# An encoder step in split fp32: values in two passes, gates normed at their banks, the second block's first weights behind its norm, the last chunk reordered

## The chip, the cores and the metric

One core of a Trainium2 chip runs the whole step as one launch. The metric is the device time of an execution in microseconds. The times are medians of several executions; a profile is of one execution.

## The reference

One layer of a streaming encoder on 512 prompt rows, 16 learned meta rows in front of them and 32 sample rows, width 1024:

```python
xp = half_step_ffn(xp, ffn1_norm, ffn1_w_gate, ffn1_w_up, ffn1_w_down)   # x + 0.5 * (silu(h@wg) * (h@wu)) @ wd
bp, cin_p, qp, ckv_p, kpe_p, gcp, gmp = project_inputs(rms_norm(xp, mix_norm), ...)  # h @ w_in_all
conv_branch = (b_gate * conv_y) @ w_conv_out
mla_branch = attn @ w_mla_out           # 16 heads, chunk-causal, keys and values expanded from 128 latents
merged = sigmoid(g_conv) * conv_branch + sigmoid(g_mla) * mla_branch
xp = xp + merged @ w_out_all
xp = half_step_ffn(xp, ffn2_norm, ...)
```

The same weights serve the sample rows (`xs`), which attend to a cache. Width of the blocks inside: 2816, heads 16 of 64 values and 96 key elements. Everything is float32, and the result must be right to nearly float32.

## The kernel before

Every float32 operand is split into a rounded part (hi) and the rest (lo): `split` casts on ScalarE and subtracts on VectorE or GpSimd. A product is three passes on TensorE (`mm3`, lines 161 to 164): hi·hi is L162, hi·lo of the moving operand L163, lo·hi L164. Activations stand with features on partitions and tokens in the free dimension, 544 or 560 columns in two halves of 272 or 280.

The stages, in order of the trace: the first feed-forward block to 384 us; its norm and the latents of keys and values to 423; attention with a filler to 935; gates, `w_mla_out` and `w_out` to 1039; the second block to the end.

A feed-forward block first makes one pair of 128-column blocks plainly (`plain`, its copies L277 and L278 empty the banks `acc`), and then 19 or 20 jobs, gate and up in turn, each of two column blocks by seven half-size products of sums (A11, A12, S2, S1, S3, A22, S4; `operands` makes the weights' sums on VectorE (tile `ws`) and casts them (`yh`, `yl`, `zh` for A22), `job` multiplies). Between the products S3 and A22 of a job the bank `b` must be read by u3, a copy with the sign changed (L385, ScalarE, tile `kept`), before A22 adds to the same bank. Between jobs stand the chunks of the down projection (`down`): `part` multiplies pairs of activations `ah`, `al`, `close` adds the result to `y`. The last chunk has three pairs, and its first two output blocks are opened before the last pair is done.

In attention each pair of heads expands keys K and values V (`expand_kv`; the keys are normed on VectorE, L976 to L984, and transposed on TensorE, L1033). Each head multiplies scores (`score`), takes the softmax (`soft`), transposes the probabilities (L1204) into four tiles pTh, pTl of 512, 384, 256 and 128 columns, and the meta rows' into `pM` (L1209, L1212 to L1214), and multiplies the values into a bank `t` (64 partitions, 512 columns), three passes a tile, and last VM by pM (L1220). L1222 copies the bank to `at`.

Beside attention runs a filler (`stream`): 48 units of 48 matmuls, each in two halves of 24 into the two `f` banks. 24 units are for the convolution, 16 for the branch gates and 8 for `w_conv_out`; `spilled` copies the last two kinds from the bank to `b1` (L903, ScalarE) and out to memory. A gate stands there without its norm R2. The late stage loads it (`gate`), multiplies by R2 on GpSimd (in three pieces, L73), takes the sigmoid (L1270), and merges both branches in `sg` (L1282, L1283), which is split into `mh` and `ml` for `w_out`.

The order on each engine is made by a scheduler that simulates the program's time line; the code's order, the buffers and added order dependencies (NoSync: on one engine, without a semaphore) are its input. So an edit at one place can change the order at others.

## Time and profile before

| | us |
|---|---|
| median of 3 executions | 1433.81 (1432.49 to 1439.06) |
| profiled execution, its own time | 1433.34 |
| its span, first to last instruction | 1431.6 |
| TensorE busy, share | 1388.9, 97% |
| VectorE busy, share | 1010.9, 71% |
| ScalarE busy, share | 650.7, 45% |
| GpSimd busy, share | 477.4, 33% |
| mean granted TensorE clock | 0.996 |

The profiled time is the span and what lies around it, 1.7 us. Busy shares are averages over stages of different kinds, and a busy TensorE is made of pipelined passes, so the distance from one start to the next tells what a pass costs.

### The profile page before, as it was taken

How to read it: one execution, taken by the hardware profiler on the slowest of the kernel's cores; microseconds unless marked ns; L12 is line 12 of the kernel's file. 1: busy time of each engine (PE TensorE's matmuls, PEld its weight loads, DVE VectorE, ACT ScalarE, POOL GpSimd, SP SyncE). 2: the span in 40 equal slices, each digit the busy share in tenths (PEclk: the TensorE clock that was granted, in tenths of full speed). 3: DMA queues.
4: the chain of work that ended last, by engine and by line, in shares of the span. 5: the costliest groups of instructions: out<-in, count | busy, mean ns of one | idle time of the engine just before them, and what ended most of it. 6: DMA issues, size and time to landing. Idle time of an engine off the chain costs nothing.

```text
span 1431.6 us, 26658 instructions
## 1 busy us (share of the span) xinstructions
PE 1388.9 (97%) x10679; PEld 1356.4 (95%) x10679; DVE 1010.9 (71%) x1708; ACT 650.7 (45%) x1218; POOL 477.4 (33%) x695
## 2 busy tenths in 40 slices
PE   7999999999999999999999999999999999999998
PEld 6999999999899999998999999998999999999998
DVE  5887877877666665956955757545977787878754
ACT  6644343535324454454554556533544343534341
POOL 1011111202286864645623424167811021111110
PEclk9999999999999999999999999999999999999999
DMA  6332323323243222222432234365442332324213
GB/s 172 89 118 73 105 76 102 103 76 90 87 123 94 84 79 77 71 61 57 120 91 72 84 115 150 110 179 165 137 117 89 89 104 74 118 75 122 67 45 96
DMA packets 215635, 141.64 MB, mean 99 GB/s; under 512 B 6415, under 2 KB 202914, under 8 KB 215510
## 3 DMA queue, kind: packets, MB, share of 16 engines
q1 hardware_dynamic: 215510, 139.93, 33.4%
q8 instruction: 84, 1.38, 0.4%
q14 instruction: 41, 0.34, 0.1%
HBM read 124.15 MB, written 15.76 MB: 98 GB/s over the span
## 4 chain that ended last, share of the span: by engine, by line
PE 82%; POOL 6%; DVE 5%; DMA 3%; issue 2%; ACT 1%; SPq 0%; POOLq 0%; ACTq 0%; DVEq 0%
PE b L162 10%; PE b L163 9%; PE b L164 9%; PE acc L162 8%; PE acc L163 8%; PE acc L164 7%; PE f L162 6%; PE f L163 6%; PE f L164 6%; POOL sg L73 2%; POOL sq L73 1%; PE t L162 1%; PE late L163 1%; PE t L1204 1%; PE late L162 1%
## 5 line engine op out<-in xcount | busy, mean ns | idle before, releaser
L73 POOL TENSOR_TENSOR al<-tu,ah 128x187 fp32r<-128x187 f32 (+3 forms) x108 | 98.5, 945 | 568.5 <-issue 340.6
L116 ACT CAST wh<-wr 128x1024 fp32r<-128x1024 f32 (+2 forms) x166 | 167.7, 1019 | 226.1 <-PE acc L163 121.1
L162 PE MATMUL f<-xh,wh 128*128 128x272 f32 (+1 forms) x816 | 240.0, 294 | 2.3 <-DVE ext L874 1.6
L164 PE MATMUL f<-xh,wl 128*128 128x272 f32 (+1 forms) x816 | 238.9, 293 | 0.0
L163 PE MATMUL f<-xl,wh 128*128 128x272 f32 (+1 forms) x816 | 238.5, 292 | 0.0
L163 PE MATMUL acc<-al,wh 128*128 128x280 f32 (+1 forms) x704 | 203.7, 291 | 3.4 <-DVE al L117 3.4
L162 PE MATMUL acc<-ah,wh 128*128 128x280 f32 (+1 forms) x704 | 203.0, 292 | 1.8 <-ACT ah L116 0.9
L164 PE MATMUL acc<-ah,wl 128*128 128x280 f32 (+1 forms) x704 | 202.8, 291 | 0.5 <-DVE wl L117 0.5
L73 POOL TENSOR_TENSOR wl<-wr,wh 128x256 fp32r<-128x256 f32 x196 | 151.8, 804 | 150.0 <-ACT wh L116 122.1
L117 DVE TENSOR_TENSOR wl<-wr,wh 128x1024 fp32r<-128x1024 f32 (+2 forms) x116 | 141.8, 1229 | 32.7 <-ACT wh L116 29.5
L162 PEld LDWEIGHTS f<-xh,wh 128*128 128x128 f32 x816 | 154.7, 190 | 3.5 <-ACT wh L116 1.8
L163 PEld LDWEIGHTS f<-xl,wh 128*128 128x128 f32 x816 | 154.7, 190 | 0.4
L164 PEld LDWEIGHTS f<-xh,wl 128*128 128x128 f32 x816 | 154.7, 190 | 0.5
L163 PEld LDWEIGHTS acc<-al,wh 128*128 128x128 f32 x704 | 132.5, 188 | 4.1 <-DVE al L117 4.0
L163 PE MATMUL b<-xsl,yh 128*128 128x272 f32 (+1 forms) x468 | 135.6, 290 | 0.0
L162 PE MATMUL b<-xsh,yh 128*128 128x272 f32 (+1 forms) x468 | 135.6, 290 | 0.0
L164 PE MATMUL b<-xsh,yl 128*128 128x272 f32 (+1 forms) x468 | 135.4, 289 | 0.0
L162 PEld LDWEIGHTS acc<-ah,wh 128*128 128x128 f32 x704 | 131.7, 188 | 3.2 <-ACT ah L116 1.4
L164 PEld LDWEIGHTS acc<-ah,wl 128*128 128x128 f32 x704 | 132.0, 188 | 0.7 <-DVE wl L117 0.7
L117 DVE TENSOR_TENSOR yl<-ws,yh 128x1024 fp32r<-128x1024 f32 x78 | 100.8, 1292 | 36.8 <-ACT yh L116 36.2
L116 ACT CAST yh<-ws 128x1024 fp32r<-128x1024 f32 x78 | 81.9, 1051 | 95.1 <-PE b L163 83.0
L467 DVE SCALAR_TENSOR_TENSOR tu<-acc,R 128x560 f32<-128x560 f32 (+1 forms) x80 | 58.2, 730 | 46.5 <-PE acc L164 46.3
(361 smaller groups left out, 3868.2 us busy)
## 6 DMA issues: line engine op xcount, KB each, us to landing
wr<-in_w_in_all_dram SPq DMA_DIRECT2D x43, 512.0 KB, 4.3
wr<-in_ffn_w_down_dram SPq DMA_DIRECT2D x32, 512.0 KB, 3.5
wr<-in_ffn_w_gate_dram SPq DMA_DIRECT2D x24, 512.0 KB, 3.8
wr<-in_ffn_w_up_dram SPq DMA_DIRECT2D x23, 512.0 KB, 5.1
wq<-in_ffn_w_up_dram SPq DMA_DIRECT2D x20, 512.0 KB, 4.2
wq<-in_ffn_w_gate_dram SPq DMA_DIRECT2D x19, 512.0 KB, 4.0
wr<-in_ffn_w_down_dram SPq DMA_DIRECT2D x16, 384.0 KB, 3.3
gt_dram<-b SPq DMA_DIRECT2D x16, 272.0 KB, 2.0
```

Source lines behind the costliest of these rows:

```text
L73: last = op(out[:, lo:hi], a[:, lo:hi], b[:, lo:hi])
L116: a = S.copy(hi, src)
L117: return a, (E or V).tensor_sub(lo, src, f(hi))
L162: PE.matmul(out, a[0], b[0], start=start, stop=False, skip_group_check=onto)
L163: PE.matmul(out, a[0], b[1], start=False, stop=False, skip_group_check=onto)
L164: PE.matmul(out, a[1], b[0], start=False, stop=stop, skip_group_check=onto)
L467: V.scalar_tensor_tensor(t, ps[:, :, :n], 0.5, Rv, op0=ALU.mult, op1=ALU.mult)
L1204: PE.transpose(ps[:, (t - j) * P : (t - j + 1) * P], pw[:, a : a + P], ident)
```

## The change

Six edits: the values' hi and lo halves lie in one tile VV, the product of a head takes two passes a tile into a bank of 128 partitions, and a ScalarE copy and a VectorE addition join the halves; the branch gates are multiplied by R2 when they leave the `f` bank, on VectorE, and not in the late stage; the second block's first summed weights get an order dependency behind the last copy of its norm (`spread` returns it; `before(1)` passes it on); the second cast of a job's weights gets one behind u3; in the first block the condition for the first job reads `combine` and not `made`; the last chunk's parts are cut at the first pair and not before the last.

```diff
--- before.py
+++ after.py
@@ -290,7 +290,7 @@
                     S.activation(g, g, AF.Silu)
                     V.tensor_mul(u, u, g)
                     split(ah[:, 0], al[:, 0], u)
-                    ready = [c(ready) for c in combine]
+                    ready = [c(ready) for c in combine] or ready
             g, u = rows(), rows()
             V.tensor_mul(two(g), ps[0][:, :, :n], Rv)
             S.activation(g, g, AF.Silu)
@@ -321,6 +321,8 @@
                 )
             return raw
 
+        made_hi = []
+
         def operands(raw, after=None):
 
             def parts(*args):
@@ -339,6 +341,7 @@
             steps.append(V.tensor_add(s2, s1, a11))
             steps.append(V.tensor_add(s4, s2, a12))
             views = A + B + parts(sums[1], pool, "y", 3) + [a22]
+            made_hi[:] = steps[-2:-1]
             if after:
                 for j, x in enumerate(steps):
                     tc.add_manual_dep(x.ins, after[j > 1].ins.name, NOSYNC, reason="later")
@@ -382,7 +385,7 @@
             product(d, S1, X1)
             product(b, S3, X3, False)
             u3 = pool.tile([P, n], F32, tag="kept", name="kept", bufs=4)
-            S.mul(u3, b, -1.0)
+            G["u3"] = S.mul(u3, b, -1.0)
             V.tensor_sub(out(0)[:, h[1]], u3, d)
             yield
             product(b, A22, X4, False)
@@ -475,9 +478,11 @@
             opened = []
             for m in range(ahead):
                 ps = open_(m)
-                part(ps, m, 0, nf - 2)
+                part(ps, m, 0, 2)
+                if m == 0:
+                    yield
+                part(ps, m, 2, nf - 2)
                 opened.append(ps)
-                yield
             for m in range(ahead):
                 part(opened[m], m, nf - 2, nf)
                 close(opened[m], m)
@@ -494,9 +499,9 @@
         jobs = [(make, w, p) for p in range(1, NF // 2) for make, w in ((gate_job, wg), (up_job, wu))]
         made = plain(0)
         ops, raws = None, [None]
-        if not made:
+        if not combine:
             raws = [fetch(*jobs[0][1:])]
-            ops = operands(raws[0])
+            ops = operands(raws[0], [made] * 2)
         raws.append(fetch(*jobs[1][1:]))
         pending = None
         ready = None
@@ -513,7 +518,9 @@
             next(g)
             pending = g
             if x + 1 < len(jobs):
-                ops = operands(raws[x + 1], made and x == 0 and made[-2:])
+                ops = operands(raws[x + 1], combine and x == 0 and made[-2:])
+                if "u3" in G:
+                    tc.add_manual_dep(made_hi[0].ins, G["u3"].ins.name, NOSYNC, reason="later")
             if x + 2 < len(jobs):
                 raws.append(fetch(*jobs[x + 2][1:]))
             if d:
@@ -896,11 +903,15 @@
                     dma(cy_dram[c], b1)
             return win(OB + c * P), META, NL, use
 
-        def spilled(w, dst):
+        def spilled(w, dst, scaled):
             def use(q, ps, x):
                 if q == 0:
                     st["b1"] = pool.tile([P, L], F32, tag="b1", name="b1")
-                S.copy(st["b1"][:, q * NL : (q + 1) * NL], ps)
+                b1 = st["b1"][:, q * NL : (q + 1) * NL]
+                if scaled:
+                    V.tensor_mul(b1, ps, R2[:, x])
+                else:
+                    S.copy(b1, ps)
                 if q == 1:
                     dma(dst, st["b1"])
             return w, META, NL, use
@@ -909,9 +920,10 @@
             units = []
             for c in range(KD):
                 units += [conv_c(c), conv_v(c), conv_b(c)]
-            units += [spilled(win(OGC + m * P), gt_dram[m]) for m in range(2 * KD)]
+            units += [spilled(win(OGC + m * P), gt_dram[m], True) for m in range(2 * KD)]
             units += [
-                spilled(i["w_conv_out"][0, :, m * P : (m + 1) * P], cb_dram[m]) for m in range(KD)
+                spilled(i["w_conv_out"][0, :, m * P : (m + 1) * P], cb_dram[m], False)
+                for m in range(KD)
             ]
             block = lambda u: load([u[0]], E=GP)
             w = block(units[0])
@@ -956,8 +968,8 @@
                 ],
             )
             K = pool.tile([P, 7, 2, QK], F32, tag="K", name="K", bufs=2)
-            Vh = pool.tile([P, 7, 2, VD], F32R, tag="Vh", name="Vh", bufs=2)
-            Vl = pool.tile([P, 7, 2, VD], F32R, tag="Vl", name="Vl", bufs=2)
+            VV = pool.tile([P, 7, 2, 2, VD], F32R, tag="VV", name="VV", bufs=2)
+            Vh, Vl = VV[:, :, :, 0], VV[:, :, :, 1]
             for t in range(7):
                 ps = bank("acc")[:, : 2 * P]
                 c = slice(t * P, (t + 1) * P)
@@ -985,7 +997,7 @@
                 K[:, :, :, NOPE:], kpe[:, :, None, :].to_broadcast([P, 7, 2, ROPE]),
                 rk[:, :, :, None].to_broadcast([P, 7, 2, ROPE]),
             )
-            return K, Vh, Vl, VM
+            return K, VV, VM
 
         def expand_q(g, us):
 
@@ -1077,7 +1089,7 @@
                 dst, src, AF.Exp, bias=nm[rows, col : col + 1], accum_out=sm[rows, col : col + 1]
             )
 
-        def sample_values(Vh, Vl, at, pS):
+        def sample_values(VV, at, pS):
 
             n = 2 * SAMP
             ps = bank("t")
@@ -1092,9 +1104,9 @@
             ov = bank("t")
             for j, (t, r) in enumerate(((5, P), (6, P), (4, SAMP))):
                 mm3(
-                    ov[:n, :P],
+                    ov[:n, :P].rearrange("p (h c) -> p h c", c=VD),
                     (sTh[:r, j], sTl[:r, j]),
-                    tuple(v[:r, t].rearrange("p h c -> p (h c)") for v in (Vh, Vl)),
+                    (VV[:r, t, :, 0], VV[:r, t, :, 1]),
                     j == 0,
                     j == 2,
                 )
@@ -1140,7 +1152,7 @@
             if e == 0:
                 at = pool.tile([P, L], F32, tag="at", name="at")
                 pS = pool.tile([P, KP], F32, tag="pS", name="pS")
-            K, Vh, Vl, VM = KV[pr]
+            K, VV, VM = KV[pr]
             pw = pws[e]
             nm = pool.tile([P, 5], F32, tag="nm", name="nm", bufs=2)
             sm = pool.tile([P, 5], F32, tag="sm", name="sm", bufs=2)
@@ -1213,15 +1225,18 @@
             V.tensor_sub(pM[32:64], ps[:32], f(pM[:32]))
             S.copy(pM[64:], ps[:32])
             fill(1.0)
-            ov = bank("t")[:VD]
+            ov = bank("t")
             for j in range(NQ):
-                vj = (Vh[:, j, e], Vl[:, j, e])
-                mm3(ov[:, 512 - NT[j] :], vj, (pTh[j], pTl[j]), j == 0, False)
-            PE.matmul(ov, VM[:, e], pM, start=False, stop=True)
+                vj = VV[:, j, e].rearrange("p s c -> p (s c)")
+                for x in (pTh[j], pTl[j]):
+                    PE.matmul(ov[:, 512 - NT[j] :], vj, x, start=j == 0 and x is pTh[j], stop=j == NQ - 1 and x is pTl[j])
+            PE.matmul(ov[:VD], VM[:, e], pM, start=False, stop=True, skip_group_check=True)
             half = slice(e * VD, (e + 1) * VD)
-            V.tensor_copy(at[half, SAMP:], ov)
+            other = slice((1 - e) * VD, (2 - e) * VD)
+            S.copy(at[half, SAMP:], ov[other])
+            V.tensor_add(at[half, SAMP:], ov[half], at[half, SAMP:])
             if e:
-                sample_values(Vh, Vl, at, pS)
+                sample_values(VV, at, pS)
                 if pr < KD - 1:
                     dma(at_dram[pr], at)
                 else:
@@ -1266,7 +1281,6 @@
         def gate(m):
             sg = late.tile([P, L], F32, tag="sg", name="sg", bufs=4)
             dma(sg, gt_dram[m])
-            GP.tensor_mul(sg, sg, R2[:, META:])
             S.activation(sg, sg, AF.Sigmoid)
             return sg
 
```

Where the instructions stand. ScalarE, in the middle of the second block: `yh` is the cast of the summed weights `ws`, `ah` that of an activation, `zh` that of A22's weights; the instruction with ACTIVATE and `kept` is u3 (L385), and the COPY to `kept` are the copies p1 and u2. Before:

```order
L365 COPY kept<-b 128x272
L116 CAST ah<-tu 128x544
L116 CAST yh<-ws 128x1024
L385 ACTIVATE kept<-b 128x272
L365 COPY kept<-b 128x272
L116 CAST zh<-wq 128x512
L389 ACTIVATE tg<-b 128x272
```

And after the change, where u3 is L388:

```order
L368 COPY kept<-b 128x272
L116 CAST ah<-tu 128x544
L388 ACTIVATE kept<-b 128x272
L116 CAST yh<-ws 128x1024
L368 COPY kept<-b 128x272
L116 CAST zh<-wq 128x512
L392 ACTIVATE tg<-b 128x272
```

The cast `yh` has moved from ahead of u3 to behind it. Between the last pass of S3 and the first of A22 on TensorE there are, over the 39 jobs, 22 to 31 passes in most; in the changed order ten jobs have 0, 0, 0, 1, 2, 2, 2, 2, 4 and 4.

VectorE at the second block's start: L336 to L340 make the weights' sums, L563, L565 (L570, L572 after) and L174 to L180 the norm, L278 empties a bank of `plain`. Before:

```order
L117 TENSOR_TENSOR zl<-wq,zh 128x512
L339 TENSOR_TENSOR ws<-ws,wr 128x512
L117 TENSOR_TENSOR yl<-ws,yh 128x1024
L340 TENSOR_TENSOR ws<-ws,wr 128x512
L336 TENSOR_TENSOR ws<-wq 128x512
L563 TENSOR_SCALAR ms<-b 128x4
L565 TENSOR_SCALAR ms<-b 32x1
L174 TENSOR_SCALAR r_77<-ms 128x5
L117 TENSOR_TENSOR yl<-ws,yh 128x1024
L178 TENSOR_TENSOR nra<-r_77 128x5
L278 COPY tu<-acc 128x544
```

After:

```order
L117 TENSOR_TENSOR zl<-wq,zh 128x512
L570 TENSOR_SCALAR ms<-b 128x4
L572 TENSOR_SCALAR ms<-b 32x1
L174 TENSOR_SCALAR r_77<-ms 128x5
L178 TENSOR_TENSOR nra<-r_77 128x5
L179 SCALAR_TENSOR_TENSOR nrb<-nra,ms 128x5
L180 SCALAR_TENSOR_TENSOR r_77<-nrb,r_77 128x5
L178 TENSOR_TENSOR nra<-r_77 128x5
L179 SCALAR_TENSOR_TENSOR nrb<-nra,ms 128x5
L278 COPY tu<-acc 128x544
```

The sums and both `yl` have moved behind the norm; L278 stands in the middle of the norm's short operations.

TensorE at the end of attention, last head: `f` are the filler's passes, `t<-ident,pw` the transpositions of the probabilities (32x128 those of the meta rows). Before:

```order
L163 MATMUL f<-xl,wh 128x272
L1204 MATMUL t<-ident,pw 128x128 x2
L164 MATMUL f<-xh,wl 128x272
L162 MATMUL f<-xh,wh 128x272
L1204 MATMUL t<-ident,pw 128x128
L163 MATMUL f<-xl,wh 128x272
...
L164 MATMUL f<-xh,wl 128x272
L1209 MATMUL t<-ident,pw 32x128 x4
L162 MATMUL t<-pTh,Vh 64x512
L163 MATMUL t<-pTl,Vh 64x512
L164 MATMUL t<-pTh,Vl 64x512
```

After:

```order
L164 MATMUL f<-xh,wl 128x272
L1216 MATMUL t<-ident,pw 128x128 x10
L1221 MATMUL t<-ident,pw 32x128 x4
L1232 MATMUL t<-pTh,VV 128x512
L1232 MATMUL t<-pTl,VV 128x512
L1232 MATMUL t<-pTh,VV 128x384
L1232 MATMUL t<-pTl,VV 128x384
```

The filler's passes between the transpositions are gone: from the values of the last head but one to the end 18 of them are left, before 70. Two passes a tile stand where three stood.

## Rows read from the trace of the kernel before

**Rows 1.** The page's first part: busy time of each engine, share of the span, instructions.

```profile
PE 1388.9 (97%) x10679; PEld 1356.4 (95%) x10679; DVE 1010.9 (71%) x1708; ACT 650.7 (45%) x1218; POOL 477.4 (33%) x695
```

**Rows 2.** The table of stretches: from and to, length, busy time and instructions of PE, PEld, DVE, ACT and POOL, granted clock of TensorE, share of the DMA engines, GB/s. The stages of attention and behind it, fifty microseconds of attention, and one microsecond behind a stop.

```profile
423.00:935.00 512.00, 503.11 (x3838) 481.81 (x3838) 336.93 (x800) 259.78 (x642) 246.24 (x393) 1.00 0.31 90
935.00:1039.00 104.00, 100.50 (x773) 99.94 (x773) 67.15 (x74) 44.95 (x60) 83.78 (x110) 0.97 0.55 161
700.00:750.00 50.00, 50.00 (x391) 47.52 (x391) 33.27 (x82) 27.18 (x77) 17.73 (x27) 1.00 0.32 94
994.00:995.00 1.00, 1.00 (x7) 1.00 (x6) 0.64 (x2) 0.00 (x0) 0.38 (x1) 0.50 0.94 286
```

**Rows 3.** The list of TensorE's waits: who waited, for what, us in all, times, longest.

```profile
PE b L162 <- ACT kept L385: 6.5, 9, 1.3
PE acc L1033 <- DVE K L984: 4.1, 2, 2.7
PE acc L163 <- DVE al L117: 3.4, 3, 1.4
PE late L162 <- ACT mh L116: 2.9, 1, 2.9
PE acc L162 <- DVE tu L278: 2.4, 1, 2.4
PE t L1220 <- ACT pM L1214: 1.5, 1, 1.5
```

**Rows 4.** The timeline of TensorE at the last head: start, duration, engine, line, operation, operands, shapes, how many. The values' passes and two groups of transpositions.

```profile
929.58 0.39 PE L164 MATMUL t<-pTh,Vl 128*64 128x512 f32 x1
929.81 0.34 PE L162 MATMUL t<-pTh,Vh 128*64 128x384 f32 x1
929.98 0.34 PE L163 MATMUL t<-pTl,Vh 128*64 128x384 f32 x1
930.57 0.28 PE L164 MATMUL t<-pTh,Vl 128*64 128x256 f32 x1
930.69 0.22 PE L162 MATMUL t<-pTh,Vh 128*64 128x128 f32 x1
930.75 0.22 PE L163 MATMUL t<-pTl,Vh 128*64 128x128 f32 x1
...
922.07 0.60 PE L1204 MATMUL t<-ident,pw 128*128 128x128 f32 x4
927.57 0.27 PE L1204 MATMUL t<-ident,pw 128*128 128x128 f32 x1
```

**Rows 5.** Groups of instructions by line and form: operands, shapes, how many, then busy us and mean ns of one, then the idle time ahead of them. Two of weight loads, two copies in attention, and a filler's eviction with the norm.

```profile
L163 PEld LDWEIGHTS t<-pTl,Vh 128*64 128x64 f32 x64 | 8.6, 135 | 2.0
L163 PEld LDWEIGHTS f<-xl,wh 128*128 128x128 f32 x816 | 154.7, 190 | 0.4
L1222 DVE COPY at<-t 64x512 f32<-64x512 f32 x16 | 10.9, 678 | 7.9 <-PE t L1220 7.5
L1212 ACT CAST pM<-t 32x512 fp32r<-32x512 f32 x16 | 9.1, 571 | 3.1 <-PE t L1209 2.9
L892 DVE TENSOR_TENSOR b<-f,R 128x272 f32<-128x272 f32 x16 | 7.0, 437 | 10.3 <-PE f L164 9.7 <-POOL VM L971 0.6
```

**Rows 6.** The timelines of GpSimd and of TensorE in the late stage (columns as in Rows 4; in brackets the idle time ahead and what ended it).

```profile
985.51 5.81 POOL L73 TENSOR_TENSOR sg<-sg,R 128x181 f32<-128x181 f32 x9
...
993.46 0.60 PE L163 MATMUL late<-ml,wh 128*128 128x272 f32 x1 [0.48 <-DVE ml L117]
993.86 0.43 PE L164 MATMUL late<-mh,wl 128*128 128x272 f32 x1
...
996.35 0.38 PE L163 MATMUL late<-ml,wh 128*128 128x272 f32 x1
```

**Rows 7.** The timelines of ScalarE and TensorE around u3, in a job of the second block and in the last job of the first.

```profile
1214.07 1.05 ACT L116 CAST yh<-ws 128x1024 fp32r<-128x1024 f32 x1 [3.59 <-PE b L163]
1215.02 0.39 ACT L385 ACTIVATE kept<-b 128x272 f32<-128x272 f32 x1
1215.46 0.39 PE L162 MATMUL b<-xsh,zh 128*128 128x272 f32 x1 [1.06 <-ACT kept L385]
...
370.33 0.28 PE L164 MATMUL b<-xsh,yl 128*128 128x280 f32 x1
371.11 0.40 PE L162 MATMUL b<-xsh,zh 128*128 128x280 f32 x1 [0.49 <-ACT kept L385]
```

**Rows 8.** The timelines of VectorE and TensorE at the second block's start.

```profile
1053.22 1.23 DVE L117 TENSOR_TENSOR yl<-ws,yh 128x1024 fp32r<-128x1024 f32 x1 [0.18 <-ACT yh L116]
1054.44 0.72 DVE L278 COPY tu<-acc 128x544 f32<-128x544 f32 x1
...
1055.21 0.39 PE L162 MATMUL acc<-xh,wh 128*128 128x272 f32 x1 [2.43 <-DVE tu L278]
```

**Rows 9.** The timelines of TensorE and VectorE around one pair's keys: the last pass of the expansion, the reduction, the last product of the keys, the first transpositions.

```profile
642.95 0.28 PE L164 MATMUL acc<-wkh,kvl 128*128 128x256 f32 x1
...
649.87 1.09 DVE L976 TENSOR_REDUCE vk<-sqk 128x14 f32<-128x896 f32 x1
...
658.80 1.14 DVE L984 TENSOR_TENSOR K<-kpe,rk 128x448 f32<-128x448 f32 x1
...
659.99 0.64 PE L1033 MATMUL acc<-ident,K 128*96 128x128 f32 x4 [2.74 <-DVE K L984]
```

## The prediction

> **What bounds the kernel now.** Read the page's list of engines first: TensorE is busy 97% of the span, VectorE 71%, ScalarE 45%, GpSimd 33% [rows 1]. Then the table by stages: TensorE stands still for 8.9 us of the 512 in the attention stage (512.00 − 503.11) and for 3.5 us of the 104 in the stage behind it [rows 2]. So the time is mostly the number of passes that TensorE makes, at about 128 ns each (50.00 us by 391 matmuls [rows 2]), and a gain is either a pass less or one of the few waits. The list of TensorE's waits gives their places: 6.5 us on the sign-changed copy u3 (`kept`, L385), 4.1 on the finished keys (L984), 2.9 on the merged rows `mh`, 2.4 on a bank's copy at the second block's start (L278), 3.4 on the last pair's `al`, 1.5 on `pM` at the end of attention [rows 3].
>
> **The change, part by part.**
>
> *Values in two passes.* The hi half and the lo half of the values stand side by side in one stationary operand, so a pass over pTh multiplies both. The pass Vh·pTl stays and brings Vl·pTl with it; the third pass (L164) goes. Start-to-start in the timeline, it takes 0.23 us at 512 columns (929.58 to 929.81), 0.17 at 384 (929.81 to 929.98), 0.12 at 256 (930.57 to 930.69) and 0.06 at 128 (930.69 to 930.75) [rows 4]: 0.58 us a head, 16 heads, −9.3 us.
> What the two left cost more: their load has 128 columns and not 64, and such loads take 190 ns against 135 [rows 5]. Behind 256 columns and more (spacing 0.12 us and up) nothing should show, since the filler's 272-column passes with 128-wide loads run at 128 ns. Behind 128 columns the nearest row is the transposition with a 128-wide operand: four take 0.60 us, one 0.27, so 0.11 us each and not 0.06 [rows 4]. Two passes, 16 heads, 0.05 us more: +1.7 us (bounds 0, if the load hides, and 1.7).
> The two halves of the result must be added: a ScalarE copy of 64x512 (nearest row 571 ns, L1212 [rows 5]) and then a VectorE add, where one VectorE copy stood (678 ns [rows 5]). The chain to `at` gets 0.6 us longer; for 15 heads nobody waits, since the bank of the values is read long after. The last head's part of it is under the tail below.
>
> *Gates take the norm at their banks.* From the late stage 48 GpSimd products go (16 gates in three pieces); nine of them take 5.81 us in a row just before the stall [rows 6], and the row `mh` waits for them through a sigmoid. In the chain of work that ended last they are what TensorE stood for: 2.9 us on `mh` [rows 3] and 0.48 more at 993.46 for `ml` [rows 6]. After that stop the granted clock is 0.50 of full, the 1.2 GHz level [rows 2]: eleven passes from 993.86 to 996.35 take 2.49 us [rows 6] where 11 × 0.128 is 1.41, so 1.1 us more. With the products gone a gate is one transfer and one sigmoid, and the merged row is ready while the row before it is multiplied. Sum −4.5 us (bounds: −3.4 if the clock falls anyway, −5.2 if the stage's other stops go too).
> The price: 32 evictions of 128x272 move from ScalarE to VectorE, 32 × 437 ns (L892 [rows 5]) = 14 us of VectorE, between some 700 and 850 us. VectorE is busy 33.27 us of 50 there [rows 2], so the work fits; but each eviction frees one of two `f` banks, and its place behind a longer operation costs when it is later than a half unit of 24 passes (3.1 us). I take +1 us (bounds 0 and 3; the 16 evictions of this kind in `before` made TensorE wait never).
>
> *The next job's second cast behind u3.* At 1214.07 ScalarE takes a 1.05 us cast `yh` and only then u3, and TensorE stops 1.06 us; at 370.33, with no cast between and no matmuls to cover it, u3 alone makes 0.78 us from start to start instead of 0.13 [rows 7]. So the stop has two parts: 0.65 us less whatever passes cover it, and the cast. The nine waits of before come to 6.5 us idle; at 371.11 start-to-start says 0.65 where idle says 0.49, so 0.16 more each, 7.9 us. In the changed order the cast is never ahead of u3 (it is in 33 of 39 jobs before). What is left is u3 alone, in jobs with few passes between S3 and A22: 0, 0, 0, 1, 2, 2, 2, 2, 4 and 4 passes, priced max(0, 0.65 − 0.128 each): 3 × 0.65 + 0.52 + 4 × 0.39 + 2 × 0.14 = 4.3 us. Sum −3.6 us (bounds −6, if the other engines let the cover stay as before, and +1, if the cast comes late for S2: about 3.1 us from its sum to its use, against at least 3.7 of cover).
>
> *Second block's first summed weights behind the norm.* At 1053.22 VectorE takes `yl` (1.23 us) ahead of the bank copy L278 at 1054.44, and TensorE stops 2.43 us for that [rows 8]. In the changed order two sums and two `yl` stand later, but the short norm operations and ScalarE's two casts remain ahead of the copies; I take −1.0 of the 2.4 (bounds −0.5 and −1.5).
>
> *Last chunk in another order.* The passes that need the last pair still follow its last S4 product with nothing between on TensorE, in both orders; the waits on `al` (3.4 us [rows 3]) stay. 0.
>
> *What moves because the rest does.* (a) Keys. From the last expansion pass (642.95) VectorE's and GpSimd's chain takes to 659.94 (reduction at 649.87, L984 from 658.80 for 1.14), and TensorE's cover is short by 2.74 us [rows 9]. Priced with row spacings, the cover of the eight pairs is 21.5, 16.9, 14.4, 14.0, 13.5, 12.3, 13.6 and 12.2 us before, and 21.5, 14.1, 14.2, 14.3, 13.5, 14.1, 14.6 and 12.5 after, with 0.4 to 1.7 us more VectorE work inside five of the chains (an eviction, an addition). The second pair, whose chain takes 16.4 us, loses 2.8 us of cover: +2.3; the pairs at the margin about +1.7. Sum +4 (bounds 0 and +8). (b) Tail. The filler ends earlier: 18 of its passes are left for the last head instead of 70, so 52 × 0.128 = 6.7 us of cover are gone there, and ten transpositions, four of `pM` and the values stand in one piece. In the bare chain (casts of pT, then `pM` in three steps of 0.57 to 0.68, then the 0.6 us copy in `at`) 1.5 us were open already [rows 3]. Sum +3 (bounds +1 and +6.7).
>
> **Sum.** −9.3 + 1.7 − 4.5 + 1 − 3.6 − 1.0 + 4 + 3 = −8.7. The profiled execution took 1433.34 us (span 1431.6), 0.5 under the median of 1433.81. 1433.34 − 8.7 = 1424.6, said as **1425 us**.
>
> **The rivals.**
> *The attention stage gives the passes back.* TensorE is 98% busy there, but keys and tail are chains of other engines, with a length of their own. For it: both lose cover in the new order. Against it: only two of eight pairs waited before. With the upper bounds of (a) and (b): 1425 + 4 + 3.7 = 1433, no change.
> *The whole gain stays.* The new waits are covered, as the 8.9 us of idle time of that stage says of most waits now. (a), (b) and evictions near 0 instead of +8: 1417; with u3's −6 1414.
> *Slower: VectorE becomes the bound between 700 and 850 us.* All gate evictions now queue behind casts' differences of up to 1.2 us on VectorE. It decides once each half unit is late by more than its two banks cover: at 0.33 us each the gain of the values is eaten (32 × 0.33 = 10.6), at 0.8 us late each it adds 26 us: some 1448. For it: 33 of 50 us busy and 14 more to come. Against: no wait on L892 in the list.
> *The weight loads set the pace.* If none of the 54 ns more of a load is hidden, 8 passes × 16 heads × 0.054 = 6.9 us in place of 1.7: 1430. Against it: passes of 272 columns hide loads of 128 columns. The Trainium skill ("TensorE: Matmul & The Clock Gate", section "LDWEIGHTS (loading the stationary operand)") speaks for it: a load's time goes by the columns of its operand alone, not by its rows, so doubling them doubles it, 53 to 107 ns by its formula. The trace agrees on the growth (135 to 190 ns), less than double.
>
> **How the numbers follow.** The forecast 0.45, own range 1420 to 1429; the whole gain 0.25; given back 0.18; loads 0.06; slower 0.06. A measurement of this kernel can tell about 0.5%, 7 us: faster means under 1426.6. Of the forecast's range two thirds lie below (0.30), all of the whole gain (0.25), and a few of the others: faster 0.57. Slower (above 1441) 0.06; same 0.37. The range 1412 to 1434 leaves out the slower case, the end of "given back" and a little below: 2 in 10.
>
> **What would show it.** Values: eight passes a head, 64 matmuls fewer, spacings 0.23, 0.17, 0.12 and 0.11; TensorE's busy time some 8 us less in the attention stage. Gates: no wait on `mh` and clock 1.00 behind 989; no wait of a filler pass on the new evictions. u3: some ten waits on `kept` of under 0.5 us, none of 1 us. Second block: L278's wait near 1.4. Keys: the wait on L984 at 8 us, tail idle 3 us longer than now. Wrong it would be if the attention stage's idle time does not grow (then 1417) or grows by more than the passes saved (then 1433 and above), or if VectorE's evictions appear among TensorE's waits.

## The result, and the profile after

The changed kernel takes 1424.8 us (median of 4 executions, 1424.04 to 1424.93) where the kernel before takes 1433.94: ratio 0.9929, interval 0.9904 to 0.9953, so 0.7% faster. The forecast was 1425. The total is right, and the profile shows that it is right for partly wrong reasons. By the forecast's terms attention was to get 0.4 us longer, and it got 4.3 shorter; the two feed-forward blocks were to give 4.6 us, and together they gave nothing. The two misses cancel. (Two executions that were very much slower than all others, 1968 us of the kernel before and 2701 us of the kernel e12 below, are left out of the medians.)

The profiled execution took 1424.04 us, its span is 1422.3. First the page's list of engines of the changed kernel, to be held against [rows 1]:

```profile
PE 1384.5 (97%) x10615; PEld 1355.5 (95%) x10615; DVE 1012.2 (71%) x1740; ACT 648.6 (46%) x1202; POOL 443.8 (31%) x647
```

64 matmuls fewer, 32 VectorE instructions more, 48 on GpSimd fewer. Then the table of stretches, cut at the first filler pass, at the first pass of `w_mla_out` and at the first pass of the second block:

```profile
0.00:423.88 423.88, 409.27 (x3084) 402.12 (x3084) 315.59 (x442) 188.13 (x285) 92.59 (x132) 1.00 0.35 102
423.88:932.05 508.17, 497.35 (x3776) 479.80 (x3777) 346.44 (x832) 259.44 (x626) 246.78 (x393) 0.99 0.31 91
932.05:1030.18 98.13, 98.13 (x770) 98.13 (x770) 62.32 (x73) 44.16 (x58) 50.37 (x61) 0.98 0.57 169
1030.18:1422.30 392.12, 379.78 (x2990) 375.48 (x2988) 287.86 (x394) 156.83 (x233) 54.02 (x63) 1.00 0.31 91
```

Cut at the same passes, the four stretches of the kernel before are 423.05, 512.44, 103.17 and 392.90 us. So attention gave 4.3 us, the late stage 5.0, the second block 0.8, and the part up to attention took 0.8 more. From the list of TensorE's waits of the changed kernel, against [rows 3] (some rows are left out):

```profile
PE b L162 <- ACT kept L388: 5.0, 14, 0.5
PE acc L163 <- DVE al L117: 3.5, 3, 1.6
PE t L1216 <- DVE pTl L117: 3.3, 2, 2.1
PE acc L162 <- ACT wh L116: 2.1, 3, 0.9
PE t L1216 <- DVE pw L1181: 1.3, 1, 1.3
PE f L162 <- DVE b L912: 1.3, 1, 1.3
PE acc L1045 <- DVE K L996: 1.1, 1, 1.1
PE t L162 <- DVE at L1237: 1.0, 1, 1.0
PE acc L162 <- DVE tu L278: 0.8, 1, 0.8
```

The wait on `mh` is gone, the one on keys nearly; the nine waits on u3 have become fourteen, shorter ones; three are new: pTl and `pw` in attention, and `b` (L912), a gate's eviction on VectorE.

**Values.** TensorE's timeline at an ordinary head, the last seven of its eight passes and the instruction behind them:

```profile
637.81 0.39 PE L1232 MATMUL t<-pTl,VV 128*128 128x512 f32 x1
638.04 0.34 PE L1232 MATMUL t<-pTh,VV 128*128 128x384 f32 x1
638.21 0.34 PE L1232 MATMUL t<-pTl,VV 128*128 128x384 f32 x1
638.39 0.28 PE L1232 MATMUL t<-pTh,VV 128*128 128x256 f32 x1
638.50 0.28 PE L1232 MATMUL t<-pTl,VV 128*128 128x256 f32 x1
638.63 0.22 PE L1232 MATMUL t<-pTh,VV 128*128 128x128 f32 x1
638.69 0.28 PE L1232 MATMUL t<-pTl,VV 128*128 128x128 f32 x1
638.80 0.33 PE L162 MATMUL s<-kTh,qTh 100*128 100x264 f32 x1
```

From start to start 0.23 us at 512 columns, 0.17, 0.11 to 0.13, 0.06, as before the change [rows 4]. Only the last pass keeps TensorE 0.11 us (638.69 to 638.80) and not 0.06.

**Keys of the fourth pair.** The last expansion pass, the reduction, the last product and the transpositions, on TensorE and VectorE:

```profile
641.32 0.28 PE L164 MATMUL acc<-wkh,kvl 128*128 128x256 f32 x1
...
646.66 1.07 DVE L988 TENSOR_REDUCE vk<-sqk 128x14 f32<-128x896 f32 x1
...
655.84 0.62 DVE L996 TENSOR_TENSOR K<-kpe,rk 128x448 f32<-128x448 f32 x1
...
657.06 0.60 PE L1045 MATMUL acc<-ident,K 128*96 128x128 f32 x4
```

The chain from 641.32 to 656.46 is 15.1 us; before it was 17.0 [rows 9]. The reduction comes 5.3 us behind the expansion instead of 6.9, and TensorE does not wait for the keys. But it waits for something else within this stretch, the differences pTl of the head beside it:

```profile
653.37 0.44 PE L1216 MATMUL t<-ident,pw 128*128 128x128 f32 x2 [1.15 <-DVE pTl L117]
```

**Second block's start.** VectorE's copy and TensorE, against [rows 8]: the stop of 2.43 us is one of 0.82.

```profile
1044.34 0.72 DVE L278 COPY tu<-acc 128x544 f32<-128x544 f32 x1 [0.28 <-PE acc L164]
1045.12 0.40 PE L162 MATMUL acc<-xh,wh 128*128 128x272 f32 x1 [0.82 <-DVE tu L278]
```

**u3.** ScalarE and TensorE in a job of the second block, against [rows 7]:

```profile
1080.47 2.00 ACT L116 CAST wh<-wr 128x1024 fp32r<-128x1024 f32 x2 [2.34 <-DMA wr<-in_ffn_w_down_dram]
1082.38 0.39 ACT L388 ACTIVATE kept<-b 128x272 f32<-128x272 f32 x1
...
1082.81 0.40 PE L162 MATMUL b<-xsh,zh 128*128 128x272 f32 x1 [0.48 <-ACT kept L388]
```

`yh` is behind u3 now. Two casts `wh`, of other weights (`w_down`), stand ahead of it, and ScalarE had stood idle for 2.34 us until their transfer landed.

**Tail of attention.** TensorE, ScalarE and VectorE at the last head:

```profile
921.11 0.93 PE L1216 MATMUL t<-ident,pw 128*128 128x128 f32 x7
924.18 0.79 PE L1216 MATMUL t<-ident,pw 128*128 128x128 f32 x3 [2.14 <-DVE pTl L117]
925.91 0.76 PE L1232 MATMUL t<-pTh,VV 128*128 128x512 f32 x1
926.46 0.63 PE L1232 MATMUL t<-pTl,VV 128*128 128x512 f32 x1
...
921.22 1.05 ACT L116 CAST wh<-wr 128x1024 fp32r<-128x1024 f32 x1 [1.11 <-issue]
922.30 1.23 DVE L117 TENSOR_TENSOR wl<-wr,wh 128x1024 fp32r<-128x1024 f32 x1 [1.52 <-ACT wh L116]
```

And stretches of the changed kernel at the last head, at the start of the late stage and in its middle, with the granted clock in the third column from the end:

```profile
927.00:928.00 1.00, 1.00 (x6) 1.00 (x5) 0.61 (x1) 0.35 (x1) 0.00 (x0) 0.50 0.01 2
934.00:935.00 1.00, 1.00 (x6) 1.00 (x5) 0.00 (x0) 0.49 (x1) 0.00 (x0) 0.50 0.05 10
985.00:990.00 5.00, 5.00 (x42) 5.00 (x41) 4.18 (x6) 1.57 (x2) 0.00 (x0) 1.00 0.37 109
```

Behind the stop at 922 the last head's values run at the 1.2 GHz level (0.55 us from 925.91 to 926.46, and not 0.31). The late stage still begins with some 3 us at half clock (the second line); in the kernel before, 936 to 938 has 0.50 too. From 937 on nothing stops and the clock is whole, where the kernel before stopped for `mh` and then ran at half clock again [rows 2, 6].

### The profile page after: what moved, and what is told of

Same layout as the page of the kernel before. It is cut to its first block, busy times and chain, and to the rows that moved or that the text cites. A ratio compares the mean times of both kernels' runs of the same rounds, so it can differ in the third digit from the quotient of the medians.

```text
span 1422.3 us, 26510 instructions
## 1 busy us (share of the span) xinstructions
PE 1384.5 (97%) x10615; PEld 1355.5 (95%) x10615; DVE 1012.2 (71%) x1740; ACT 648.6 (46%) x1202; POOL 443.8 (31%) x647
## 4 chain that ended last, share of the span: by engine, by line
PE 82%; DVE 6%; DMA 3%; POOL 3%; ACT 2%; issue 2%; SPq 0%; POOLq 0%; DVEq 0%; ACTq 0%
PE b L162 8%; PE b L163 8%; PE b L164 8%; PE acc L162 8%; PE acc L164 8%; PE acc L163 8%; PE f L162 6%; PE f L163 6%; PE f L164 6%; PE late L164 2%; PE late L162 2%; PE late L163 2%; DMA wr<-in_ffn_w_down_dram 2%; PE t L1232 1%; POOL sq L73 1%
## 5 line engine op out<-in xcount | busy, mean ns | idle before, releaser
L117 DVE TENSOR_TENSOR wl<-wr,wh 128x1024 fp32r<-128x1024 f32 (+2 forms) x116 | 138.3, 1202 | 42.6 <-ACT wh L116 35.2
L116 ACT CAST yh<-ws 128x1024 fp32r<-128x1024 f32 x78 | 81.5, 1045 | 19.9 <-PE b L163 15.5
L162 PE MATMUL b<-xh,wh 128*128 128x272 f32 (+1 forms) x312 | 90.5, 290 | 0.0
```

What stands on the lines that cost most here:

```text
L116: a = S.copy(hi, src)
L117: return a, (E or V).tensor_sub(lo, src, f(hi))
L162: PE.matmul(out, a[0], b[0], start=start, stop=False, skip_group_check=onto)
```

## The experiments

Each kernel was timed against the kernel before on the same chip, where the kernel before took 1433.6 to 1434.7 us. In the table: the median, the ratio, and from the profiled execution the four stretches cut as above. Where two kernels of the table are compared, the ratios are the better measure, since the chips differ.

| kernel | median us | ratio (interval) | to attention | attention | late | second block |
|---|---|---|---|---|---|---|
| before | 1433.94 | | 423.1 | 512.4 | 103.2 | 392.9 |
| changed | 1424.80 | 0.9929 (0.9904, 0.9953) | 423.9 | 508.2 | 98.1 | 392.1 |
| e1 values alone | 1430.51 | 0.9970 (0.9960, 0.9980) | 425.4 | 508.1 | 102.5 | 393.5 |
| e2 gates alone | 1431.18 | 0.9977 (0.9967, 0.9986) | 424.6 | 514.0 | 98.6 | 392.3 |
| e3 order behind u3 alone | 1439.99 | 1.0045 (1.0028, 1.0062) | 424.1 | 512.2 | 106.1 | 395.3 |
| e4 norm first alone | 1432.67 | 0.9985 (0.9975, 0.9994) | 422.8 | 510.9 | 103.1 | 391.2 |
| e9 changed, no order behind u3 | 1422.89 | 0.9926 (0.9911, 0.9940) | 423.8 | 507.6 | 98.1 | 392.1 |
| e6 changed + cover | 1420.49 | 0.9913 (0.9898, 0.9928) | 421.7 | 507.6 | 97.9 | 390.5 |
| e7 changed + tail | 1422.67 | 0.9924 (0.9908, 0.9941) | 423.3 | 506.0 | 98.5 | 393.8 |
| e8 changed + cover + tail | 1418.58 | 0.9894 (0.9878, 0.9911) | 420.6 | 506.1 | 98.5 | 391.3 |
| e10 as e8, no order behind u3 | 1424.37 | 0.9927 (0.9912, 0.9942) | 422.0 | 506.9 | 98.9 | 394.6 |
| e11 changed, gates as before | 1433.33 | 0.9993 (0.9983, 1.0002) | 423.1 | 510.8 | 106.4 | 393.0 |
| e12 changed, last chunk as before | 1424.69 | 0.9932 (0.9915, 0.9949) | 424.7 | 508.4 | 98.4 | 392.5 |
| e13 changed again | 1423.97 | 0.9921 (0.9905, 0.9938) | 425.2 | 506.6 | 98.3 | 394.1 |

The rows of the changed kernel and of e13 are the same program: a stretch of one profile differs by up to 2 us from that of another. So stretches are read together with the waits in them.

**e1, values alone.** The hunks on VV, `sample_values` and the head's end, on the kernel before:

```diff
-            Vh = pool.tile([P, 7, 2, VD], F32R, tag="Vh", name="Vh", bufs=2)
-            Vl = pool.tile([P, 7, 2, VD], F32R, tag="Vl", name="Vl", bufs=2)
+            VV = pool.tile([P, 7, 2, 2, VD], F32R, tag="VV", name="VV", bufs=2)
...
```

> The kernel before with the values in two passes alone. Theory A (the sum of the prediction): the passes saved are given back by keys and tail, -9.3 + 1.7 + 4 + 3 = about -0.6 us: 1433 us, the attention stage (first filler pass to first pass of w_mla_out, 512.4 us before) at 512. Theory B (from the changed kernel's trace, where 128-wide loads cost 0.05 us a head and the waits on keys fell from 4.1 to 1.1 us): the passes are worth 8.5 us and the other engines' chains take at most 3 of it back: 1426 to 1429 us, the stage at 504 to 508.

Attention is 508.1 us, 4.4 shorter, and the kernel 0.3% faster: theory B on the stage. The key chains are those of the changed kernel (the second pair 14.2 us, the fourth 15.1, where before has 16.4 and 17.0), so the shorter chains came with the values and not with the gates. The total is 1430.5, above theory B's 1426 to 1429. What its profile shows beside is a wait of 2.6 us on `xh` in attention, with half clock behind it (858 to 861), and half clock at 28 to 31 and at 384 to 386, all three at whole clock in the kernel before.

**e2, gates alone.** `spilled(..., True)` for the gates and no product in `gate`, on the kernel before.

> The kernel before with the gates normed at their banks alone. Theory A: late stage -4.5 us, evictions on VectorE +1: 1430 us. Theory B: the late stage gives its whole stop and the slow clock behind it, -5 us (103.2 to 98.1), and one or two filler passes wait 1.3 us each for an eviction on VectorE: 1430 us too, but with a wait of filler passes on the banks in the list. A rival C: the attention stage gets longer by more than 3 us, VectorE being late at many evictions: 1432 or more.

The late stage falls by 4.5 us, attention grows by 1.6: the two terms of the prediction, and less than rival C's 3. Theory B's wait is in the list, once, with 0.7 us (in the changed kernel 1.3):

```profile
PE f L162 <- DVE b L905: 0.7, 1, 0.7
```

**e3, the order behind u3 alone.**

```diff
+            made_hi[:] = steps[-2:-1]
...
+            G["u3"] = S.mul(u3, b, -1.0)
...
+                if "u3" in G:
+                    tc.add_manual_dep(made_hi[0].ins, G["u3"].ins.name, NOSYNC, reason="later")
```

> The kernel before with one order dependency alone: the second cast of a job's weights behind u3 (on ScalarE). Theory A: the waits on kept fall from 7.9 us start-to-start to about 4.3: -3.6 us, 1430 us. Theory B (from the changed kernel's trace, where a cast of other weights, wh, stands ahead of u3 in five jobs): another cast takes the place, the waits on kept stay above 6 us: 1433 us within 1.

Neither: 6 us slower. The waits on u3 are 5.2 us in 13, not 6.5 in 9 (start to start some 0.7 us less), but the block around them is 2.4 us longer and the late stage 2.9: there the wait on `mh` is 4.4 us instead of 2.9.

```profile
PE late L162 <- ACT mh L116: 4.4, 1, 4.4
```

Behind this stop the granted clock is 0.50 for twice as long as in the kernel before (995 to 1001 throughout, where the kernel before is whole again from 997 on), and 1060 to 1064 has 0.69, where the kernel before has nothing of the kind. Why the late stage's stop grew, which this edit does not touch but the scheduler lays anew, stays open; e11 has it again.

**e4, norm first alone.** `ops = operands(raws[0], [made] * 2)` with what hands `made` on.

> The kernel before with the second block's first summed weights behind its norm alone. Theory A: L278's stop falls by 1.0 of 2.4 us: 1433 us. Theory B: by 1.6 us as in the changed kernel's trace: 1432 us. Neither: the sums come late for the first job's S products and a new wait of over 1 us on yh or yl appears in the first two jobs.

The second block gives 1.7 us: theory B; 0.15% (interval 0.06 to 0.25).

**e9, the changed kernel without the order behind u3.** The last two lines of e3's diff are taken out.

> The changed kernel without the order dependency of the second cast behind u3. Theory A (the prediction's sum): +3.6 us, 1428. Theory B (the dependency only changes which cast stands ahead of u3, 7.9 us of stops against 7.3): within 1.5 us of the changed kernel, and the waits on kept are those of the kernel before, nine of 6.5 us.

Theory B. The list says for this kernel what [rows 3] says for the one before, and the two blocks take 0.1 us less than with it:

```profile
PE b L162 <- ACT kept L388: 6.5, 9, 1.3
```

In the whole change this edit is worth nothing that can be seen.

**e6, cover for u3.** On TensorE the next job's A12, or a down chunk's first block, is held behind S3:

```diff
-            product(c, A12, B21)
+            product(c, A12, B21, after=G.get("s3"))
...
-            product(b, S3, X3, False)
+            G["s3"] = product(b, S3, X3, False)
...
+                        if (m, j, q) == (0, 0, 0) and not last:
+                            tc.add_manual_dep(first.ins, G["s3"].ins.name, NOSYNC, reason="cover")
```

> The changed kernel, and on TensorE the next job's A12 product (or the first block of a down chunk) held behind this job's S3 by an order dependency, so that at least 6 passes, mostly 12 or 24, stand between S3 and A22. Theory A (u3's stop is a matter of the passes left as cover, whatever stands on ScalarE): the waits on kept fall from 7.3 us start-to-start to under 2, and the time by about 5 us to 1420. Theory B (the passes were used earlier because something else was late there, so the idle time only moves): new waits of 3 us and more on yh, yl or wh in the jobs, and 1425 us within 1.5.

Theory A in the time: 1420.5, 4.3 us under the changed kernel by medians and 2.3 by ratios, whose intervals overlap. In the waits it is half right: the fourteen become four, and start to start they fall from 7.3 us to 4.0, not to under 2:

```profile
PE b L162 <- ACT kept L393: 2.9, 4, 1.9
```

The longest, 1.9 us ahead of 1079, stands behind 12 passes of cover. It has two casts `wh` ahead of u3, which had waited 2.6 us for their transfer; the others have `wh` ahead of u3 too. The passes had not been used where something else was late: no wait on yh or yl took the place.

**e7, the tail.** The third weight block of the late stage is cast behind the last head's end:

```diff
-            ps = project(i["w_mla_out"][0, :, m * P : (m + 1) * P], (vh, vl))
+            ps = project(i["w_mla_out"][0, :, m * P : (m + 1) * P], (vh, vl), after=tail if m == 2 else None)
```

> The changed kernel with the third weight block of the late stage cast behind the last head (its cast wh at 921 us and difference wl at 922 stand ahead of pTh and pTl of the last head in the changed kernel). Theory A (these two make TensorE's stop of 2.4 us in the tail, and the stop brings the slow clock behind it): the tail's stop at the transpositions goes to under 0.5 us, and with it the stretch at half clock over the last values: -3 to -4 us, 1421. Theory B (the chain of pTh, pTl and pM alone is that long without filler): the stop only moves to pM: 1424 to 1425 us.

In the profile in between, nearer to theory B: the stop at the transpositions is halved (1.07 us for 2.14) and not ended, one on `pM` appears, and the half clock comes all the same, over 924 to 932. The time is 2.1 us lower by medians and 0.7 by ratios, which is not clear of the noise. TensorE's timeline:

```profile
920.98 0.79 PE L1220 MATMUL t<-ident,pw 128*128 128x128 f32 x3 [1.07 <-DVE pTl L117]
922.34 0.61 PE L1225 MATMUL t<-ident,pw 128*32 128x128 f32 x4 [0.57 <-DVE pTl L117]
924.99 0.69 PE L1237 MATMUL t<-pM,VM 96*64 96x512 f32 x1 [0.24 <-ACT pM L1230]
```

**e8, both.**

> Both of the last two on the changed kernel. If both of their theories A hold: 1416 to 1418 us. If one holds: 1420 to 1421. If none: 1425.

1418.6 us, ratio 0.9894 (0.9878 to 0.9911), just above what both theories A gave: it beats both kernels, by 5 us (ratios) the changed one, all of whose executions are slower than all of these, and by 15 the one before. How much of it each edit gives is less sure: by medians the two gains add (4.3 and 2.1), by ratios the single gains are 2.3 and 0.7.

**e10, as e8 without the order behind u3.**

> The kernel with the cover and the tail's order, without the order dependency of the second cast behind u3. Theory A (u3's stop goes by cover and cast together): most jobs have 12 passes, 1.5 us, in both, so the cast ahead of u3 costs at most 0.2 us a job: within 1.5 us of the run with the dependency, 1417 to 1420. Theory B (the dependency is worth the 3.6 us of the prediction once other things are right): 1421 or more.

Theory B in the time: slower than with it by 4.7 us (ratios), of which the profiles show 3.3 in the second block. u3's own stops are not what differs. With `yh` ahead of u3 the longest is 2.5 us, but e8 has one of 2.0, and start to start they come to 4.7 us in both. The list of e8:

```profile
PE b L165 <- ACT kept L396: 3.6, 4, 2.0
```

And that of this kernel, where a wait comes up that no other kernel here has, on `yl`:

```profile
PE b L165 <- ACT kept L396: 4.0, 4, 2.5
PE b L167 <- DVE yl L117: 2.7, 4, 1.2
```

So in time the order behind u3 is worth nothing without the cover (e9) and some 5 us with it, and as far as the profiles show it pays by the wait on `yl`, which is absent with it, and not by shorter stops on u3. Why `yl` comes late without it stays open.

**e11, the changed kernel with the gates as before.**

> The changed kernel with the gates back as before (evictions on ScalarE, products with the norm on GpSimd in the late stage). Theory A (the prediction's terms, -4.5 and +1): 1428 to 1429, the late stage at 102 to 103 us again with a wait on mh and the half clock behind it, the attention stage 1 us shorter. Theory B (with fewer passes in the stage VectorE's evictions cost more than alone): the attention stage 3 us shorter, 1426.

Neither: 1433.3 us, so the gates' edit carries nearly the whole gain in company, where alone it gave 0.23%. Against the changed kernel the late stage is 8.3 us longer, and attention 2.7 longer, not shorter.

```profile
PE late L162 <- ACT mh L116: 4.3, 1, 4.3
```

The late stage is that of e3, which has the order behind u3 and the gates as before, as this kernel has: 106.4 and 106.1 us, a wait of 4.3 and 4.4 on `mh`, and half clock for twice as long behind it (here 993 to 999 throughout). Kernels with the gates as before and without that order have 102.5 to 103.2 (before, e1, e4), all with the gates at their banks 97.9 to 98.9. So the order behind u3 costs some 3 us in the late stage, and the gates' edit removes the stop that it makes longer. For attention, TensorE, ScalarE and two stretches of this kernel, the last in the late stage:

```profile
857.51 0.82 PE L162 MATMUL f<-xh,wh 128*128 128x272 f32 x2 [3.24 <-ACT xh L116]
856.82 0.64 ACT L116 CAST xh<-raw 128x544 fp32r<-128x544 f32 x1 [4.14 <-DMA raw<-cy_dram]
857.00:859.00 2.00, 1.49 (x5) 1.23 (x6) 1.51 (x4) 2.00 (x9) 0.61 (x1) 0.50 0.00 0
994.00:996.00 2.00, 2.00 (x9) 2.00 (x10) 1.91 (x3) 0.65 (x1) 0.00 (x0) 0.50 0.19 57
```

ScalarE stands 4.1 us on a reload of the convolution's rows, with work behind it that TensorE needs; the filler's next unit waits 3.2 us and runs at half clock after it. e1 has the same wait (2.6 us on `xh`). In the changed kernel ScalarE stands 2.5 us on this reload too (the cast at 856.37), but TensorE has other passes there and waits only 0.2 us. That it is the gates' order on ScalarE that makes the difference is an inference, since the whole order differs.

**e12, the changed kernel with the last chunk as before.**

> The changed kernel with the last chunk's parts cut as before. The prediction's term is 0: within 0.7 us of the changed kernel, the waits on al unchanged at 3.5 us. Against it: the cut moves the first pair's passes ahead of the last job's A22, so without it that job's stop on kept falls or grows by up to 0.7 us, twice.

1424.7 against 1424.0 for the changed kernel beside it, with intervals that overlap; the waits on `al` are 3.4 us in both. The term of 0 holds.

**e13, the changed kernel again.**

> The changed kernel itself, beside these. 1424 to 1425 us; half-clock stretches at the same three places as in its first profile if they belong to the program's stops, at other places if they come from one execution to the next.

The time holds. The half clock in the tail and at the start of the late stage is there again, but the third place changed: 384 to 388, the first line, has 0.70 here, and 1.00 in the first profile, the second line, which has its half clock at 424 instead.

```profile
384.00:388.00 4.00, 4.00 (x24) 4.00 (x24) 4.00 (x6) 1.42 (x2) 2.83 (x4) 0.70 0.58 185
```

```profile
384.00:388.00 4.00, 4.00 (x33) 4.00 (x33) 4.00 (x6) 2.09 (x3) 3.42 (x5) 1.00 0.73 245
```

The same program after the same stops (0.97 and 1.55 us on `al`): 24 passes in four microseconds, or 33. The stops on u3 are not the same either. They come to 6.3 us where the first profile has 5.0, and start to start to 8.5 and not 7.3:

```profile
PE b L162 <- ACT kept L388: 6.3, 14, 1.1
```

The longest stands behind a cast `wh` whose transfer landed late:

```profile
1341.30 1.05 ACT L116 CAST wh<-wr 128x1024 fp32r<-128x1024 f32 x1 [2.16 <-DMA wr<-in_ffn_w_up_dram]
```

In the first profile the same cast waited 1.17 us for its transfer, and A22 started 0.52 us behind the pass before it; here it is 1.42.

## Why the prediction was right, and where it was not

| term | forecast | measured | how |
|---|---|---|---|
| third pass | −9.3 | −9.3 | 64 passes fewer, spacing of the others unchanged |
| loads of 128 columns | +1.7 | +0.8 | 0.05 us on the last pass of a head, 16 heads |
| late stage | −4.5 | −5.0 | 103.2 to 98.1 |
| evictions on VectorE | +1 | +1.3 | one wait on L912 |
| u3 | −3.6 | −0.6 | 7.9 to 7.3 us, start to start (8.5 in e13) |
| second block's start | −1.0 | −1.6 | L278's wait 2.43 to 0.82 |
| last chunk | 0 | 0 | e12 |
| keys | +4 | −3.0 | the wait 4.1 to 1.1; with the pTl stop inside it −1.8 |
| tail | +3 | +2.8 | below |
| not in the sum | | some +4 | pTl 1.2 and `pw` 1.3 in attention; `wh` 0.8; start 0.8 |

**Right by its mechanism.** The passes: each size cost what the timeline said. The late stage: its stop and the half clock behind it went together, and without the products there is no other stop. Second block: right in kind, a little small (its bounds ended at −1.5). The gates' price on VectorE: one wait, 1.3 us, near the term of +1; the prediction's last part named such a wait as a sign of being wrong, against its own sum. The forecast of attention's idle time did not hold: it went from 9.0 to 10.8 us, where the terms +1, +4 and +3 ask for some 8 more.

**The tail: right in size, in part by luck.** The stops of 2.14 and 0.56 on pTl, 0.98 on `at` and 0.35 make 4.0 us where before had 2.4 (`pM` 1.46, 0.55, 0.35); +1.7, and the values there, 2.37 us from 925.91 to 928.28 where an ordinary head takes 1.30, +1.1 of half clock. So the stops grew by little more than half of the +3, and a half clock that no term had made up the rest. The lost cover is not the whole reason either: `wh` and `wl` of a later stage stand ahead of pTh and pTl, and without them (e7) the stops are 3.2 us.

**Wrong: u3.** The step that failed is "what is left is u3 alone". For a bare u3 the formula held to 0.01 us: 0.65 with no pass between (three jobs), 0.52 with one, 0.39 with two (four jobs), 0.14 with four. But in six other jobs two `wh` casts of 1 us each stand directly ahead of u3, where `yh` stood, and ScalarE had waited 1.0 to 2.3 us for their transfer before it could begin them. These jobs have 4, 11 or 12 passes between, the formula gave them 0.14 in all, and they cost 3.2 us (0.64 at 1082, behind 11 passes). I had looked for the cast that stood there before, and not for what the queue puts in its place, nor for the transfer that this waits for. When the transfer lands differs from one execution to the next, and the stop with it (e13), so −0.6 is the figure of one profile; by e13's it would be +0.6. e9 shows the edit worth 0 here. e6 shows both halves apart: its jobs of few passes, now with 6 to 12, have no stop any more, and all that is left (4.0 us start to start) is in jobs with `wh` ahead. No run moved these casts or their transfers, so their share is read from the traces alone.

**Wrong: keys.** The step that failed carried the chains' lengths over from the old trace and changed only the cover. The cover was right: without the stops in them, the second, third and fourth pair have 14.4, 14.4 and 14.6 us, against 14.1, 14.2 and 14.3 in the forecast. The chains were not: 16.4, 16.4 and 17.0 us became 14.2, 15.5 and 15.1. The part ahead of the reduction became shorter by some 1.6 us in the second and the fourth pair (6.8 to 5.1 and 6.9 to 5.3). e1 shows the same chains with the values alone. It was VectorE's order that set the reduction's start, not ScalarE's copies or GpSimd's squares: in these pairs the last squares (`sqk`) were done 1.7 to 3.5 us ahead of it in both kernels. In the second pair the copy L1222 (0.65 us) and a maximum `nm` (0.45) of one head stood ahead of the reduction before and no longer do, while 0.44 us of the filler's (`c`) came in; for the fourth the share of each operation stays open. Not all of the 3.0 us is a gain: 1.15 of them stand as the stop on pTl in the fourth pair's stretch.

**The total** came out at 1425 since keys were 7 us too dear and u3 3 us too cheap, with some 4 us of small waits that no term had. That these cancel was luck. (The measured terms sum to some −10.6; the spans differ by 9.3, and the stretches at half clock that move between executions are larger than the rest.) The rival "the whole gain stays" (1417) was refuted by these waits and the tail, "given back" by the keys, the weight loads by 0.8 us of 6.9, and VectorE's bound by one wait of 1.3 us in 32 evictions.

**Not additive.** e1, e2 and e4 alone give 0.30, 0.23 and 0.15%, together 0.68, and e9, which holds just these and the last chunk, gives 0.74: these add. The order behind u3 does not: alone it costs 0.45% (e3), in the whole nothing (e9). And the gates taken from the whole (e11 beside e13) cost 0.7%, three times what they gave alone. Of that, the larger part is the late stage, 8.3 us between the profiles, of which 5 are the gates' own and some 3 are what the order behind u3 adds where the gates are as before; the rest is the reload of `xh` in attention, for which TensorE waits long in the two kernels with values in two passes and gates as before (e1, e11).

## What to carry to other kernels

When an instruction is moved out of the way on an in-order queue, look at what the queue puts in its place, at whether that waits for a transfer, and at how many passes cover the wait; here the order paid (some 5 us) only after the cover was held. A chain's length belongs to one order as much as its cover does, so neither can be carried over alone. And judge an edit both alone and in company, since where orders are laid anew the price of one depends on the others.

## What was not expected of the hardware

A stop of TensorE can cost more than its length. Behind some stops the granted clock was 0.50, the 1.2 GHz level, for some 3 us or twice that, at 0.23 us a pass and not 0.127, so 1.1 to 1.7 us on top for 3 us of it: behind `mh` (2.9 us) in the kernel before, behind pTl (2.1 us) in the changed one, behind `xh` (3.2 us) in e11. Behind others it stayed whole: in the kernel before the 2.7 us on keys at 660 and the 2.4 on L278 at 1055 were followed by 4 us at 1.00. It is not bound to one place: the same program had it at 384 us in one execution and at 424 in another. That the clock depends on how busy the array has been is what the Trainium skill says ("TensorE: Matmul & The Clock Gate", Part 1, on the clock gate); the traces agree on the fall behind some stops, and show the exceptions above.

Loads of twice the columns took 197 ns instead of 135 and were hidden at all sizes from 256 columns up and, with 128 columns, for one pass of two: 0.05 us a head remains.
